# Gains applied at the split, weight splits ordered behind the norm chain, and fp32 GLU units in a hybrid S5 / latent-attention trunk

## The chip, the cores and the metric

The kernel runs on one core of one Trainium2 chip, as one launch. The metric is the device time of that launch in microseconds. The core has five engines with their own instruction queues: TensorE (PE in the profile, with its weight loads listed as PEld), VectorE (DVE), ScalarE (ACT), GpSimd (POOL) and SyncE (SP), which issues the DMA transfers. Each engine works through its queue in order.

## The reference

A residual stream x of 256 tokens by 2048 channels, fp32, goes through four sub-layers, each between two RMS norms with their own gains ("sandwich" norms):

```
x = x + norm(s5(norm(x, g00)), g01)      # state space, then a GLU: val * sigmoid(gate)
x = x + norm(ffn0(norm(x, g02)), g03)    # 2048 -> 5632 -> 2048, gated, causal conv of width 3
x = x + norm(attention(norm(x, g10), K/V from norm(x, kv_norm_g)), g11)
x = x + norm(ffn1(norm(x, g12)), g13)
```

with `norm(x, g) = x * rsqrt(mean(x*x) + 1e-6) * g`. The state-space mixer is a complex diagonal recurrence (128 groups of 16 channels, 64 states each) over the 256 tokens, a gelu, and `y @ w_glu + b_glu`, of which one half gates the other. The attention is a latent attention with 16 heads, rank 512 for queries and keys/values and a rotary part, masked by chunks of 64 tokens. All weights come as fp32 and are read once.

## The kernel before

The 256 tokens are two blocks of 128 (tb = 0 and 1). **Weight units.** Weights stream from HBM in units of 1 MB (`wunit`, L76): a transfer into `raw` (two buffers), then two halves of 128 x 1024, each split into a high and a low fp32r part: ACT copies the high part (L73, `whi`), DVE subtracts it from the fp32 value (L74, `wlo`). For a weight with a gain, L101 does the same per row. The units that span a change of stage go to named slots (`HOLD`, tiles `x...`) instead of the rotating `whi`/`wlo`. A product is three fp32r matmuls (`mm3`, L107 to L110: high x high, high x low, low x high) or two (`mm2`, L114, L115). Activations are split in the same way (`act` tiles, the transposed layout with channels on partitions, tokens in the free dimension).

**Stages.** The state-space stage (`s5`, until about 262 us) is a software pipeline over 16 state blocks: per block PE makes small products (L399, L467, L481, L497), DVE multiplies and runs the scan (L508), ACT copies out of PSUM. After every fourth block `part_d` (L545) turns four channel tiles of the result y and splits them; they are one quarter (`qt`) of the GLU's contraction. Each finished quarter puts four GLU weight units (`glu_early`, L243: two column blocks x two halves) into the list `todo`, and each later step of the pipeline takes one of them. What is left of the list, and the column blocks 2 and 3, run in `glu_rest` (L624). Then come `ffn(0)` (L684), `attention` (L818), `ffn(1)`.

**The change of stage.** When a stage ends, each token block goes through a chain. `finish_chunk` (L163) takes the sum of squares on ACT (L139) and multiplies the result f by the post-norm's gain on DVE (L166), four times 512 columns. `post_norm` (L168) makes the reciprocal root (`rstd1`, L141: sum L145, power on POOL L147, and three small DVE rows L149, L151, L153), adds to the residual (L172, four times), squares it (L139), and, where the next stage is an FFN, multiplies x by the next norm's gain into f (L178, four times). `pre_scale` (L180) makes a second reciprocal root and scales the identity by it (L182, tile `xh`). `pre_turn` (L185) turns the block by 16 fp32 matmuls with `xh` as the moving operand (L191), so that the norm's scale is applied by the turn itself, and splits the result (L192). The turn of block 0 runs before the next stage's first products; the turn of block 1 (`tail()`) runs after block 0's products of the first four (or, for the attention, held) units. The gain is a broadcast load of 1 MB (`gb`, L160).

**What sets the order.** The program is written in one order; a scheduler puts each engine's instructions into a fixed queue by the order of the program and by when their inputs would be ready in its model. So splits of the next stage's weights stand between the small rows of the chain on DVE.

Of the kernel before, what the change touches and what calls it, by code (L numbers as in the profile page):

```python
# [15 lines left out]
P = 128  # L16
D = 2048
# [27 lines left out]
def tile_trunk(ctx: ExitStack, tc: tile.TileContext, a: dict):  # L45
# [117 lines left out]
    def finish_chunk(f, fst, tb, n, g):  # L163
        c = f[tb][:, n * 512 : (n + 1) * 512]
        sq_acc(c, fst[tb][:, n : n + 1])
        dve.tensor_tensor(c, c, g[0][:, n * 512 : (n + 1) * 512], op=ALU.mult)  # L166

    def post_norm(f, fst, tb, x, xst, g):  # L168
        r = rstd1(fst[tb], D)
        for n in range(NCH):  # L170
            c = slice(n * 512, (n + 1) * 512)
            dve.scalar_tensor_tensor(x[tb][:, c], f[tb][:, c], r, x[tb][:, c], op0=ALU.mult, op1=ALU.add)  # L172
            if xst is None:
                sync.dma_start(a["out"][tb * P : (tb + 1) * P, c], x[tb][:, c])
                continue
            sq_acc(x[tb][:, c], xst[:, n : n + 1])
            if g is not None:
                dve.tensor_tensor(f[tb][:, c], x[tb][:, c], g[0][:, c], op=ALU.mult)  # L178

    def pre_scale(xst):  # L180
        d = T(env["ap"], [P, 512], F32, "xh", 2)[:, :P]
        dve.tensor_scalar(d, ident, rstd1(xst, D), None, op0=ALU.mult)  # L182
        return d

    def pre_turn(h, d, tb):  # L185
        for n in range(NCH):
            pt = accb()
            ptv = pt.rearrange("p (k t) -> p k t", t=P)
            for k in range(4):
                o = (4 * n + k) * P  # L190
                pe.matmul(ptv[:, k, :], h[:, o : o + P], d, start=True, stop=True)  # L191
            split(*acts4(tb, n, slice(0, 4)), ptv)  # L192

# [42 lines left out]
    def glu_mm(bank, b, tb, halves):  # L236
        hk, u = halves
        for i, (wh, wl) in enumerate(u):
            for k in range(hk):
                j = i * hk + k  # L240
                mm3(bank, *acts(tb, 4 * b + j), wh[:, k, :], wl[:, k, :], b == 0 and j == 0, b == 3 and j == 3)

    def glu_early(f, n, b, half):  # L243
        hv = glu_load(n, b, half)
        banks = [accb(), accb()]
        for tb in range(NB):
            hk, u = hv
            for i, (wh, wl) in enumerate(u):
                for k in range(hk):
                    j = i * hk + k  # L250
                    mm3(banks[tb], *acts(tb, 4 * b + j), wh[:, k, :], wl[:, k, :], j == 0, j == 3)
        o = half * 1024 + n * 512
        for tb in range(NB):
            c = f[tb][:, o : o + 512]
            if b == 0:
                act.activation(c, banks[tb], AF.Copy)
            else:
                dve.tensor_tensor(c, banks[tb], c, op=ALU.add)


    def s5(f):
        with tc.tile_pool(name="s5", bufs=2) as q1:
# [276 lines left out]

            def glu_steps(b):  # L540
                for n in range(2):
                    for half in range(2):
                        yield glu_early(f, n, b, half)

            def part_d(qt, yg):  # L545
                act_tiles()
                for hh in range(2):
                    ptv = wk().rearrange("p (t m) -> p t m", t=4)
                    for t in range(4):
                        pe.transpose(ptv[:, t, :], yg[:, 7 - (4 * hh + t), :], ident)  # L550

                    def av(z):
                        return z.rearrange("p j (c t) -> p t j c", t=8)[:, 4 * hh : 4 * hh + 4]

                    for tb in range(NB):
                        hi, lo = acts4(tb, qt, slice(0, 4))
                        split(av(hi), av(lo), ptv.rearrange("p t (j c) -> p t j c", j=4)[:, :, :, 16 * tb : 16 * tb + 16])

# [18 lines left out]
            for n in range(nb + 2):  # L577
                if 0 <= n - 1 < nb:
                    vs = part_v(U[n - 1], ET.pop(n - 1))
                if n >= 2:  # L580
                    m = n - 2
                    if m % PB == 0:
                        yg = T(q1, [P, 8, P], F32, "yg", 1)
                    part_c(m, yg, ab.pop(m)[1], U.pop(m), TP.pop(m), H.pop(m))
                if 0 <= n - 1 < nb:
                    R = part_r(n - 1, vs, *fr[n - 1])
                if n < nb:
                    U[n], TP[n] = part_k(n, *ab[n])
                    ET[n] = part_e(ab[n][0])
                if 0 <= n - 1 < nb:  # L590
                    H[n - 1] = part_h(n - 1, R, *fr.pop(n - 1))
                if n >= 2 and m % PB == PB - 1:
                    part_d(m // PB, yg)
                    todo.append(glu_steps(m // PB))
# [9 lines left out]
    sync.dma_start(gkv, a["gkv"])  # L604
    sync.dma_start(gq, a["gq"])
# [17 lines left out]

    def glu_rest(q1, todo, f, fst, gains, done):  # L624
        def finish(n, tb, banks, bb):
# [6 lines left out]
            dve.tensor_tensor(c, c, sg, op=ALU.mult)  # L632
            finish_chunk(f, fst, tb, n, gains[0])

# [11 lines left out]
        for n in range(2, 4):  # L646
            banks = [(wk if n % 2 == 0 else accb)() for _ in range(4)]
            held = []
            for b in range(4):
# [9 lines left out]
                if n == 2 and b < 2:  # L659
                    if b == 0:  # L660
                        gain_load(gains[0])
                    bb = bias(b)
                    for tb in range(NB):
                        finish(b, tb, None, bb)
                if n == 2 and b == 2:
                    load_x(x)
                if n == 3 and b == 0:
                    bb = bias(2)
                    for tb in range(NB):
                        finish(2, tb, pb, bb)  # L670
                    gain_load(gains[1])
# [12 lines left out]
    def ffn(l, tail, gains, f, fst, done):  # L684
        with tc.tile_pool(name=f"ff{l}", bufs=2) as q1:
# [42 lines left out]
            for part, npair in enumerate(PARTS):  # L728
                hid = []
                for pr in range(p0, p0 + npair):  # L730
                    banks = [wk(), wk()] if pr == 0 else [[wk(), wk()] for _ in range(2)]
                    held = []
                    for which, w in enumerate((wg, wu)):
                        for kh in range(2):
                            v = w[:, 8 * kh : 8 * kh + 8, pr * S : (pr + 1) * S]
                            if pr == 0:
                                held.append((which, kh, wunit(v, 8, S, slots=HOLD[len(held)])))
                            else:
# [36 lines left out]
                if part == len(PARTS) - 2:  # L775
                    for g in gains:
                        if g is not None:
                            gain_load(g)

# [4 lines left out]
                def evac(n, tb, bank):  # L784
# [5 lines left out]
                    if last:  # L790
                        finish_chunk(f, fst, tb, n, gains[0])

# [24 lines left out]

    def attention(tail, gains, f, fst, done):  # L818
        with tc.tile_pool(name="at", bufs=2) as q1:
# [34 lines left out]
            for which, (w, gain) in enumerate(((wdkv, gkv), (wdq, gq))):  # L854
                banks = [accb(), accb()]
                held = []
                for un in range(4):
                    hv = wunit(
                        w[:, 4 * un : 4 * un + 4, 0:RANK], 4, RANK, gain[:, 4 * un : 4 * un + 4],
                        slots=(None, None) if which else HOLD[un],  # L860
                    )
                    down(banks[0], un, 0, hv)
# [156 lines left out]

            for g in gains:  # L1020
                gain_load(g)
            for n in range(NCH):
# [8 lines left out]
                for tb in range(NB):  # L1031
# [6 lines left out]
                    act.activation(c, banks[tb], AF.Copy)  # L1038
                    finish_chunk(f, fst, tb, n, gains[0])
                    if held:  # L1040
# [19 lines left out]
    def begin(gpost, gpre, last=False, f=None):  # L1060
        f, fst, xst = f or f_pair(), [stats() for _ in range(NB)], [None if last else stats() for _ in range(NB)]
        gp = gain_tile(gpost)
        gn = None if gpre is None else gain_tile(gpre)

        dg = {}

        def done(tb, stage):
            if stage == 0:
                post_norm(f, fst, tb, x, xst[tb], gn)
# [5 lines left out]
        return (gp, gn), f, fst, done  # L1075

    with tc.tile_pool(name="gl", bufs=2) as q1:
        gs, f, fst, done = begin(ng[0, 1], ng[0, 2], f=f)
        tail = glu_rest(q1, todo, f, fst, gs, done)
        rope_tables(q1)  # L1080
    tail = ffn(0, tail, *begin(ng[0, 3], None))
    tail = attention(tail, *begin(ng[1, 1], ng[1, 2]))
    ffn(1, tail, *begin(ng[1, 3], None, True))


# [28 lines left out]
def _arrays(i):  # L1114
# [8 lines left out]
    def blocks(re, im):  # L1123
# [21 lines left out]
        "w_glu": g("ssm_w_glu")[0],  # L1145
        "b_glu": g("ssm_b_glu"),
        "gkv": pn(g("kv_norm_g")),
        "gq": pn(g("norm_g")[1, 0]),
# [30 lines left out]
```

## Time and profile before

| | |
|---|---|
| median of three runs | 2193.63 us (2193.27 to 2194.26) |
| profiled execution | 2187.58 us |
| its span, first to last instruction | 2185.8 us |
| mean granted TensorE clock | 0.990 |
| busy: PE, DVE, ACT | 2079.0 us (95%), 1408.8 us (64%), 1122.4 us (51%) |
| DMA | 374.74 MB, mean 171 GB/s |

A row of the order of time gives start, duration, engine, line, operation, `out<-in`, shapes, a count, and in brackets the idle time before it and what released it. A group row gives busy time, mean ns and the idle time before. A released wait names the last semaphore that came. An fp32 matmul stands in the records as two (x2 per matmul), so 16 matmuls of the turn are x32.

### The profile page before, as it was taken

Reading aid. Unit: us, or ns where it says so; the run is one execution under the profiler, and the core shown is the slowest. Engines: PE = TensorE matmul, PEld = TensorE weight load, DVE = VectorE, ACT = ScalarE, POOL = GpSimd, SP = SyncE. Lnnn points to the kernel's source line nnn. Section 1 sums busy time; section 2 is a strip of 40 time slices with the busy share of each in tenths; the row PEclk is TensorE's granted clock in tenths of the full one; section 3 lists DMA queues with packets and bytes.
Section 4 is the critical chain, followed back from the end, with each engine's and each line's share of the span. In section 5 each row is a group of like instructions: output and inputs, shape, how many; then the busy total and the mean of one; then the engine's idle time right before and its main releaser. Section 6 shows DMA issues by size and latency. Waiting matters only on the chain.

```text
span 2185.8 us, 32404 instructions
## 1 busy us (share of the span) xinstructions
PE 2079.0 (95%) x13268; PEld 1764.2 (81%) x13268; DVE 1408.8 (64%) x1940; ACT 1122.4 (51%) x1695; POOL 19.8 (1%) x57
## 2 busy tenths in 40 slices
PE   3788999899999999999989999989999999999998
PEld 2566777888888888888878998788888888888886
DVE  7999666666466556655686665566646655665567
ACT  6677445455455445544464554545545544554444
POOL 0000000000000000000000000000000000000000
PEclk9999999999999999999999999999999999999999
DMA  4132476455565555555564434635555555555654
GB/s 131 50 98 75 154 233 206 145 188 179 193 197 187 193 193 191 178 190 193 192 200 129 136 118 155 212 123 189 189 193 193 180 187 193 193 183 184 194 191 154
DMA packets 280966, 374.74 MB, mean 171 GB/s; under 512 B 9200, under 2 KB 196208, under 8 KB 279792
## 3 DMA queue, kind: packets, MB, share of 16 engines
q1 hardware_dynamic: 280816, 372.66, 52.4%
q8 instruction: 104, 1.70, 0.3%
q14 instruction: 46, 0.38, 0.1%
HBM read 370.54 MB, written 2.10 MB: 170 GB/s over the span
## 4 chain that ended last, share of the span: by engine, by line
PE 82%; DVE 10%; DMA 4%; ACT 3%; issue 1%; POOL 0%; SPq 0%; DVEq 0%; POOLq 0%; ACTq 0%
PE wk L114 29%; PE wk L115 15%; PE acc L108 9%; PE acc L109 9%; PE acc L110 9%; DMA raw<-in_w_glu 3%; PE wk L108 2%; PE wk L109 2%; PE wk L110 2%; DVE wlo L74 2%; PE acc L191 1%; DVE x L74 1%; ACT whi L73 1%; DVE f L431 1%; DVE f L430 1%
## 5 line engine op out<-in xcount | busy, mean ns | idle before, releaser
L74 DVE TENSOR_TENSOR wlo<-raw,whi 128x1024 fp32r<-128x1024 f32 (+2 forms) x640 | 761.0, 1191 | 584.0 <-ACT whi L73 579.3
L73 ACT ACTIVATE whi<-raw 128x1024 fp32r<-128x1024 f32 (+2 forms) x640 | 658.3, 1031 | 635.3 <-PE wk L114 245.6
L114 PE MATMUL wk<-act,whi 128*128 128x512 f32 x2688 | 941.9, 395 | 0.0
L115 PE MATMUL wk<-act,wlo 128*128 128x256 f32 x2688 | 753.0, 280 | 0.0
L114 PEld LDWEIGHTS wk<-act,whi 128*128 128x128 f32 x2688 | 504.1, 188 | 119.3
L115 PEld LDWEIGHTS wk<-act,wlo 128*128 128x128 f32 x2688 | 507.4, 189 | 0.3
L108 PE MATMUL acc<-whi,hh 128*128 128x512 f32 x652 | 255.4, 392 | 0.0
L109 PE MATMUL acc<-wlo,hh 128*128 128x512 f32 x652 | 255.3, 392 | 0.0
L110 PE MATMUL acc<-whi,hl 128*128 128x512 f32 x652 | 254.3, 391 | 0.0
L108 PEld LDWEIGHTS acc<-whi,hh 128*128 128x128 f32 x652 | 122.4, 188 | 27.2 <-ACT hh L73 0.5
L109 PEld LDWEIGHTS acc<-wlo,hh 128*128 128x128 f32 x652 | 122.4, 188 | 27.0 <-DVE wlo L74 0.5
L110 PEld LDWEIGHTS acc<-whi,hl 128*128 128x128 f32 x652 | 122.4, 188 | 26.9
L108 PE MATMUL acc<-whi,act 128*128 128x512 f32 (+1 forms) x332 | 126.4, 381 | 2.7 <-ACT act L73 2.7
L109 PE MATMUL acc<-wlo,act 128*128 128x512 f32 (+1 forms) x332 | 124.9, 377 | 1.9 <-DVE wlo L74 1.9
L110 PE MATMUL acc<-whi,act 128*128 128x512 f32 (+1 forms) x332 | 124.3, 375 | 0.1
L765 DVE SCALAR_TENSOR_TENSOR cv<-gs,cw,cv 128x255 f32<-128x255 f32 (+1 forms) x168 | 77.2, 480 | 3.0
L109 PEld LDWEIGHTS acc<-wlo,act 128*128 128x128 f32 x332 | 62.5, 188 | 14.9 <-DVE wlo L74 4.0
L108 PEld LDWEIGHTS acc<-whi,act 128*128 128x128 f32 x332 | 62.5, 188 | 14.5 <-ACT act L73 3.0
L110 PEld LDWEIGHTS acc<-whi,act 128*128 128x128 f32 x332 | 62.5, 188 | 11.5 <-DVE act L74 0.5
L763 ACT ACTIVATE cv<-gs,cb,cw 128x256 f32<-128x256 f32 x84 | 50.5, 601 | 36.5 <-DVE gs L715 36.5
L714 ACT ACTIVATE us<-wk 128x256 f32<-128x256 f32 x84 | 31.7, 380 | 60.3 <-PE wk L115 60.3
L714 ACT ACTIVATE gs<-wk 128x256 f32<-128x256 f32 x84 | 32.0, 381 | 59.8 <-PE wk L115 59.8
(282 smaller groups left out, 2342.5 us busy)
## 6 DMA issues: line engine op xcount, KB each, us to landing
raw<-in_w_gate SPq DMA_DIRECT2D x88, 1024.0 KB, 5.0
raw<-in_w_up SPq DMA_DIRECT2D x88, 1024.0 KB, 4.9
raw<-in_w_down SPq DMA_DIRECT2D x88, 1024.0 KB, 4.9
raw<-in_w_glu SPq DMA_DIRECT2D x32, 1024.0 KB, 6.2
raw<-in_w_o SPq DMA_DIRECT2D x16, 1024.0 KB, 4.9
raw<-in_w_ukv SPq DMA_DIRECT2D x8, 1024.0 KB, 5.3
gb<-in_norm_g SPq DMA_DIRECT2D x6, 1024.0 KB, 6.7
raw<-in_w_uq SPq DMA_DIRECT2D x8, 768.0 KB, 4.4
```

The costliest lines, as they stand in the source:

```text
L73: act.activation(hi, src, AF.Copy)
L74: (eng or dve).tensor_tensor(lo, src, hi.bitcast(F32), op=ALU.subtract)
L108: pe.matmul(o, lh, rh, start=first, stop=False)
L109: pe.matmul(o, lh, rl, start=False, stop=False)
L110: pe.matmul(o, ll, rh, start=False, stop=last)
L114: pe.matmul(ov, lh, r, start=first, stop=False)
L115: pe.matmul(ov[:, 0, :], ll, r[:, 0, :], start=False, stop=last)
L191: pe.matmul(ptv[:, k, :], h[:, o : o + P], d, start=True, stop=True)
L430: dve.tensor_tensor(f1, zt(0, 0, 9, 1), bc(2, 9), op=ALU.mult)
L714: act.activation(z[:, ft, :], two[ft][:, S:], AF.Copy)
L763: act.activation(cv[:, ft, :], gv[:, ft, :], AF.Identity, scale=cw[:, 2, n : n + 1], bias=cb[:, n : n + 1])
L765: dve.scalar_tensor_tensor(cv[:, ft, sh:], gv[:, ft, : S - sh], cw[:, 2 - sh, n : n + 1], cv[:, ft, sh:], op0=ALU.mult, op1=ALU.add,)
```

## The change

Three things change.

1. The next norm's gain is no longer multiplied into f ahead of the turn. x itself is turned in every case, and for the two FFNs the gain, now a per-partition scalar (`gf`, 128 x 16, loaded at the start of the program), is applied when the turned block is split: 16 ACT copies with a scale and 16 DVE `scalar_tensor_tensor` of 128 x 128 for each token block, in place of four and four of 128 x 512. The broadcast gain loads of these two norms go.
2. `behind(ins)` orders what is issued in it behind the instruction that scales the identity for block 0 (on the same engine, DVE): the post-gain multiply of block 1, the end of the GLU of block 1, and the low splits of the next stage's first units (in the FFN all but the first of the held four, in the attention the third and fourth of the first weight).
3. The GLU units of the first three quarters (12 of the 16 in `todo`) are not split. `glu_full` multiplies the raw fp32 weights with an fp32 copy of the turned activations (`ax`, one more ACT copy in `part_d`): 8 fp32 matmuls of 512 columns in place of 24 fp32r. The fourth quarter's stay split.

```diff
@@ finish_chunk, post_norm, pre_scale, pre_turn
-        dve.tensor_tensor(c, c, g[0][:, n * 512 : (n + 1) * 512], op=ALU.mult)
+        with behind(env["turn"] if tb else None):
+            dve.tensor_tensor(c, c, g[0][:, n * 512 : (n + 1) * 512], op=ALU.mult)
...
-            if g is not None:
-                dve.tensor_tensor(f[tb][:, c], x[tb][:, c], g[0][:, c], op=ALU.mult)
...
+    def behind(ins):
+        return nullcontext() if ins is None else tc.issue_after(ins)
+
+    def pre_turn(h, d, tb, g):
...
-            split(*acts4(tb, n, slice(0, 4)), ptv)
+            hi, lo = acts4(tb, n, slice(0, 4))
+            if g is None:
+                split(hi, lo, ptv)
+                continue
+            for k in range(4):
+                gk = g[:, 4 * n + k : 4 * n + k + 1]
+                act.activation(hi[:, k, :], ptv[:, k, :], AF.Copy, scale=gk)
+                dve.scalar_tensor_tensor(
+                    lo[:, k, :], ptv[:, k, :], gk, hi[:, k, :].bitcast(F32), op0=ALU.mult, op1=ALU.subtract
+                )
@@ new
+    def glu_full(f, n, b, half, ax):
+        raw = T(env["wp"], [P, 4, 512], F32, "raw")
+        col = half * D + n * 512
+        sync.dma_start(raw, glu_w[b][:, :, col : col + 512])
+        banks = [accb(), accb()]
+        for tb in range(NB):
+            for j in range(4):
+                pe.matmul(banks[tb], ax[:, j, tb * P : (tb + 1) * P], raw[:, j, :], start=j == 0, stop=j == 3)
+        glu_keep(f, n, b, half, banks)
@@ part_d, glu_steps
+                        yield glu_early(f, n, b, half) if ax is None else glu_full(f, n, b, half, ax)
...
+                ax = None if qt == 3 else T(q1, [P, 4, S], F32, "ax", 1)
...
+                        if ax is not None:
+                            act.activation(av(ax[:, :, tb * P : (tb + 1) * P]), src, AF.Copy)
@@ program start
+    gf = [T(cp, [P, KT], F32, f"gf{l}") for l in range(2)]
+    for l in range(2):
+        sync.dma_start(gf[l], a["gf"][l])
@@ glu_rest, ffn, attention
-            finish(3, tb, banks, bb)
+            with behind(env["turn"] if tb else None):
+                finish(3, tb, banks, bb)
...
-                                held.append((which, kh, wunit(v, 8, S, slots=HOLD[len(held)])))
+                                with behind(before if held else None):
+                                    held.append((which, kh, wunit(v, 8, S, slots=HOLD[len(held)])))
...
+                    with behind(before if which == 0 and un > 1 else None):
@@ begin
+        env["turn"] = None
...
-                    dg[tb] = pre_scale(xst[tb])
+                    dg[tb], ins = pre_scale(xst[tb])
+                    if tb == 0:
+                        env["turn"] = ins
             elif not last:
-                pre_turn((x if gn is None else f)[tb], dg[tb], tb)
+                pre_turn(x[tb], dg[tb], tb, gpre)
```

The lines of the new kernel are shifted: L145 to L153 stay, L166 becomes L167, L172 becomes L173, L182 becomes L181, L629 and L631 become L660 and L662; L201 is the new low split with the gain, L261 the fp32 matmul.

DVE's queue at the change from the GLU to `ffn(0)`, from block 0's first reciprocal root to its `xh` (`x_...` and `wlo` are low splits of the FFN's first units, `tot` the sum of squares, `sg` the gate of block 1). Before:

```order
L145 TENSOR_REDUCE tot_4044<-st_597_3290 128x1
L74 TENSOR_TENSOR x_792_4262<-raw_4260,x_792_4262 128x1024
...
L74 TENSOR_TENSOR x_793_4265<-raw_4260,x_793_4265 128x1024
L153 SCALAR_TENSOR_TENSOR rs_r_741_4052<-rs_u_740_4050,rs_y_738_4046 128x1
L172 SCALAR_TENSOR_TENSOR x_3285<-f_84,rs_r_741_4052,x_3285 128x512 x2
L178 TENSOR_TENSOR f_84<-x_3285,gb_3295 128x512 x2
...
L74 TENSOR_TENSOR x_795_4270<-raw_4268,x_795_4270 128x1024
...
L74 TENSOR_TENSOR wlo_4274<-raw_4268,whi_4273 128x1024
L153 SCALAR_TENSOR_TENSOR rs_r_751_4080<-rs_u_750_4078,rs_y_748_4074 128x1
L166 TENSOR_TENSOR f_85<-f_85,gb_3294 128x512
L182 TENSOR_SCALAR xh_4070<-cst_73,rs_r_751_4080 128x128
```

And in the changed kernel:

```order
L145 TENSOR_REDUCE tot_3773<-st_558_3045 128x1
L149 TENSOR_SCALAR rs_m_695_3777<-tot_3773 128x1
L151 SCALAR_TENSOR_TENSOR rs_u_696_3779<-rs_m_695_3777,rs_y_694_3775 128x1
L153 SCALAR_TENSOR_TENSOR rs_r_697_3781<-rs_u_696_3779,rs_y_694_3775 128x1
L173 SCALAR_TENSOR_TENSOR x_3040<-f_88,rs_r_697_3781,x_3040 128x512 x4
L145 TENSOR_REDUCE tot_3797<-st_560_3047 128x1
...
L181 TENSOR_SCALAR xh_3795<-cst_73,rs_r_707_3805 128x128
L660 TENSOR_TENSOR sg_3920<-acc_3536,bias_3624 128x512
L74 TENSOR_TENSOR x_748_4007<-raw_4005,x_748_4007 128x1024
L662 TENSOR_TENSOR f_89<-acc_3534,bias_3624 128x512
L201 SCALAR_TENSOR_TENSOR act_220_1125<-acc_3868,gf_6_78,act_220_1125 128x128
```

The chain of block 0 now stands alone up to `xh`; the low splits, block 1's bias rows and the 16 new gain splits come behind it and ahead of block 1's own `xh`.

ACT's queue near the start of the state-space stage (`whi` are high splits of the first GLU units, `TP` and `vs` copies that the pipeline's next products read). Before:

```order
L73 ACTIVATE whi_1167<-raw_1165 128x1024
L419 ACTIVATE bc_469<-bc_469,cst_73 128x128
L73 ACTIVATE whi_1171<-raw_1165 128x1024
L73 ACTIVATE whi_1355<-raw_1353 128x1024
L473 ACTIVATE TP_288<-acc_289 128x512
```

And in the changed kernel:

```order
L506 ACTIVATE ET_329<-wk_336 128x512
L443 ACTIVATE bc_473<-bc_473,cst_73 128x128
L497 ACTIVATE TP_292<-acc_293 128x512
L497 ACTIVATE TP_292<-acc_294 128x512
L512 ACTIVATE vs_376<-wk_367 128x2x128
```

The three splits that stood ahead of the copies are gone with the units' split form.

More of the change, by code (lines that the diff above doesn't have):

```diff
@@ L1 @@
 import math
-from contextlib import ExitStack
+from contextlib import ExitStack, nullcontext
 import concourse.bass as bass
@@ L251, in glu_early, with glu_keep @@
                     mm3(banks[tb], *acts(tb, 4 * b + j), wh[:, k, :], wl[:, k, :], j == 0, j == 3)
+        glu_keep(f, n, b, half, banks)
+    def glu_keep(f, n, b, half, banks):
         o = half * 1024 + n * 512
@@ L622, in rope_tables, with glu_rest @@
         sincos(rsin, rcos, rr, rn, cst[:, C_RS : C_RS + 1])
-    def glu_rest(q1, todo, f, fst, gains, done):
+    def glu_rest(q1, todo, f, fst, gain, done):
         def finish(n, tb, banks, bb):
@@ L632, in finish @@
             dve.tensor_tensor(c, c, sg, op=ALU.mult)
-            finish_chunk(f, fst, tb, n, gains[0])
+            finish_chunk(f, fst, tb, n, gain)
         def bias(n):
@@ L660, in glu_rest @@
                     if b == 0:
-                        gain_load(gains[0])
+                        gain_load(gain)
                     bb = bias(b)
@@ L670, in glu_rest @@
                         finish(2, tb, pb, bb)
-                    gain_load(gains[1])
                     bb = bias(n)
@@ L678, in glu_rest, with ffn @@
                 done(0, 1)
-            finish(3, tb, banks, bb)
+            with behind(env["turn"] if tb else None):
+                finish(3, tb, banks, bb)
             done(tb, 0)
         return lambda: done(1, 1)
-    def ffn(l, tail, gains, f, fst, done):
+    def ffn(l, tail, before, gain, f, fst, done):
         with tc.tile_pool(name=f"ff{l}", bufs=2) as q1:
@@ L775, in ffn @@
                 if part == len(PARTS) - 2:
-                    for g in gains:
-                        if g is not None:
-                            gain_load(g)
+                    gain_load(gain)
                 def load(n, un, slots=(None, None)):
@@ L790, in evac @@
                     if last:
-                        finish_chunk(f, fst, tb, n, gains[0])
+                        finish_chunk(f, fst, tb, n, gain)
                 if last:
@@ L815, in ffn, with attention @@
         return lambda: done(1, 1)
-    def attention(tail, gains, f, fst, done):
+    def attention(tail, before, gpost, f, fst, done):
         with tc.tile_pool(name="at", bufs=2) as q1:
@@ L857, in attention @@
                 for un in range(4):
[L858 to L861, printed above, removed]
+                    with behind(before if which == 0 and un > 1 else None):
+                        hv = wunit(
+                            w[:, 4 * un : 4 * un + 4, 0:RANK], 4, RANK, gain[:, 4 * un : 4 * un + 4],
+                            slots=(None, None) if which else HOLD[un],
+                        )
                     down(banks[0], un, 0, hv)
@@ L1018, in attention @@
                     q = {"kv": kv, "qn": qn, "qr": rope(q1, qs_, br[:, S:])}
-            for g in gains:
-                gain_load(g)
+            gain_load(gpost)
             for n in range(NCH):
@@ L1038, in attention @@
                     act.activation(c, banks[tb], AF.Copy)
-                    finish_chunk(f, fst, tb, n, gains[0])
+                    finish_chunk(f, fst, tb, n, gpost)
                     if held:
@@ L1146, in _arrays @@
         "b_glu": g("ssm_b_glu"),
+        "gf": np.stack([pn(g("norm_g")[l, 2]) for l in range(2)]),
         "gkv": pn(g("kv_norm_g")),
```

30 lines of the change are left out of this document (14 added, 16 removed).

## The prediction

> **What bounds the kernel now.** I first read the page's chain of waits, then the busy time by stretches, then each engine's order of time where a stretch has gaps. All times are of the profiled execution (2187.58 us); the median of the runs is 2193.63 us, so the sum below is a difference that I add to the median.
>
> The chain that ended last, shares of the span:
>
> ```profile
> PE 82%; DVE 10%; DMA 4%; ACT 3%; issue 1%; POOL 0%; SPq 0%; DVEq 0%; POOLq 0%; ACTq 0%
> ```
>
> TensorE (PE) carries the span; the other 18% lie in few places. Stretches from 93 us on (columns: from:to, length, then busy us and count of PE, PE weight load, DVE, ACT, POOL, then granted clock, DMA share, GB/s):
>
> ```profile
> 93.00:235.00 142.00, 122.89 (x1993) 93.14 (x1999) 132.21 (x211) 105.64 (x197) 0.25 (x4) 1.00 0.28 79
> 235.00:262.00 27.00, 26.81 (x277) 21.36 (x262) 16.57 (x26) 11.67 (x18) 0.00 (x0) 1.00 0.43 132
> 262.00:300.00 38.00, 34.78 (x146) 26.67 (x145) 29.69 (x38) 18.31 (x25) 0.00 (x0) 0.99 0.87 289
> 300.00:386.00 86.00, 83.51 (x351) 65.78 (x349) 52.38 (x64) 41.63 (x51) 0.59 (x2) 0.98 0.68 204
> 386.00:432.00 46.00, 38.74 (x294) 37.82 (x295) 26.99 (x49) 19.04 (x35) 3.54 (x5) 0.89 0.38 131
> ...
> 40.00:50.00 10.00, 5.55 (x60) 4.12 (x68) 6.55 (x11) 5.18 (x14) 0.00 (x0) 0.67 0.25 72
> 390.00:400.00 10.00, 6.76 (x38) 6.76 (x39) 9.78 (x20) 4.64 (x11) 2.28 (x3) 0.58 0.70 243
> 1140.00:1150.00 10.00, 4.66 (x24) 4.66 (x25) 9.89 (x23) 8.53 (x22) 1.98 (x4) 0.66 0.77 217
> 1420.00:1430.00 10.00, 2.60 (x12) 2.02 (x11) 9.86 (x20) 5.29 (x12) 2.83 (x3) 0.79 0.40 138
> ```
>
> In the state-space stage (93 to 235) DVE is busy 132.2 of 142 us and PE idles 19.1: both engines are near the bound, DVE nearer. From 235 to 386 PE idles 0.2 + 3.2 + 2.5 us. Each of the three changes of stage holds a hole: around 395, 1145 and 1425 DVE is full (9.8 to 9.9 of 10) while PE waits, and the granted clock drops to 0.58, 0.66 and 0.79. The rows of PE that end these holes, and the turn of the second token block:
>
> ```profile
> 393.24 6.28 PE L191 MATMUL acc<-xh,f 128*128 128x128 f32 x32 [7.29 <-DVE xh L182]
> 410.76 3.73 PE L191 MATMUL acc<-xh,f 128*128 128x128 f32 x32
> ...
> 1145.34 4.82 PE L191 MATMUL acc<-xh,x 128*128 128x128 f32 x24 [5.92 <-DVE xh L182]
> ...
> 1428.87 5.61 PE L191 MATMUL acc<-xh,f 128*128 128x128 f32 x32 [7.41 <-DVE xh L182]
> ```
>
> 7.29, 5.92 and 7.41 us of waiting for the scaled identity xh. The turn behind the first takes 6.28 us for 32 records, the second turn 3.73: the half clock costs another 2.5.
>
> **Part 1: the fp32 units.** Twelve GLU units drop two ACT and two DVE splits each and issue 8 fp32 matmuls in place of 24. What they issue now in 93 to 235 (groups by line: busy, mean ns, idle before), and how closely matmuls follow each other, split form at 265 us and fp32 form in the scores at 1227 us:
>
> ```profile
> L108 PE MATMUL acc<-whi,act 128*128 128x512 f32 x64 | 26.4, 412 | 2.7 <-ACT act L73 2.7
> ...
> L74 DVE TENSOR_TENSOR wlo<-raw,whi 128x1024 fp32r<-128x1024 f32 x16 | 19.4, 1220 | 4.3 <-ACT whi L73 4.3
> L73 ACT ACTIVATE whi<-raw 128x1024 fp32r<-128x1024 f32 x16 | 16.8, 1053 | 5.6 <-PE acc L110 5.6
> ```
>
> ```profile
> 265.10 0.39 PE L108 MATMUL acc<-whi,act 128*128 128x512 f32 x1
> ...
> 265.78 0.39 PE L108 MATMUL acc<-whi,act 128*128 128x512 f32 x1
> ...
> 1226.68 0.60 PE L951 MATMUL acc<-knT,qnT 128*128 128x256 f32 x2
> 1227.11 0.59 PE L952 MATMUL acc<-krE,rpo 128*128 128x256 f32 x2
> ```
>
> Three split matmuls take 265.78 - 265.10 = 0.68 us, so a unit 8 x 0.68 = 5.45. One fp32 matmul of 256 columns takes 1227.11 - 1226.68 = 0.43 us, of 512 then 0.86, a unit 6.9. That is +1.45 per unit. No row has an fp32 matmul of 512 columns; the nearest by form, the turn's 3.73 us for 16 matmuls of 128 columns, gives 0.93 per 512, so +1.45 to +2.0; I take the wider rows, 1.45. [...]
>
> 64 L108 in 93 to 235 are 8 units: PE rises there by 8 x 1.45 = 11.6 to 134.5; DVE falls by 19.4 to 112.8; ACT loses 16.8 and gains some 3 for the copy ax. The bound goes from DVE's 132 to PE's 134.5, and what decides is how much of PE's 19.1 us of idle is left. Those waits hang on DVE and ACT results that now come sooner. If 10 us stay, the stretch is 144.5, **+2.5**. Ends: 5 left, -2.5; all 19.1 left, +11.6.
>
> At the start of the stage ACT stands in its fixed order before work that PE wants:
>
> ```profile
> 42.09 1.06 ACT L73 ACTIVATE whi<-raw 128x1024 fp32r<-128x1024 f32 x1 [1.90 <-DMA raw<-in_w_glu]
> 43.05 1.07 ACT L473 ACTIVATE TP<-acc 128x512 f32<-128x512 f32 x2
> ...
> 44.45 0.48 PE L497 MATMUL wk<-cst,vs 128*128 128x128 f32 x1 [5.46 <-ACT vs L488]
> ```
>
> The weight split of 42.09, waiting for its transfer, stands ahead of the copy TP, and PE waits 5.46 us for what follows. The split is gone; DVE, busy 6.55 of 10 us there, can win back up to 3.45. I take -3.0, +0.9 for the two gain loads put at the head of SP's queue (issues there are 0.44 apart), and -0.6 for ACT's four splits in all that leave this place: **-2.7** (ends -4 and +0.9).
>
> ```profile
> 0.74 0.38 SPq L604 DMA_DIRECT2D gkv<-in_gkv  x1
> 1.18 0.41 SPq L605 DMA_DIRECT2D gq<-in_gq  x1
> ```
>
> From 235 on PE is full, so the other four fp32 units cost 4 x 1.45 = 5.8. One more thing comes: an fp32 unit reads raw until its last matmul, and there are two raw buffers, so the next transfer starts up to 6.9 us later, and the quarter behind it must again fill the split path. ACT already waits there for transfers:
>
> ```profile
> L73 ACT ACTIVATE whi<-raw 128x1024 fp32r<-128x1024 f32 x38 | 40.1, 1058 | 55.4 <-DMA raw<-in_w_glu 30.8 <-PE acc L110 15.2 <-PE wk L110 9.4
> ```
>
> One split pair, 1.05 + 1.22, is the refill: +2.3, and up to 5 with the transfer. Against it, 20 units between 265 and 386 take 121 us where 20 x 5.45 = 109 would do; an earlier start of transfers can give back some of these 12. I take 5.8 + 2.3 - 5.7 = **+2.4** (ends -4 and +11).
>
> **Part 2: gains at the split and the order behind xh.** At the first change of stage, DVE and GpSimd (POOL) stand so:
>
> ```profile
> 381.99 0.21 DVE L151 SCALAR_TENSOR_TENSOR rs_u<-rs_m,rs_y 128x1 f32<-128x1 f32 x1
> ...
> 383.44 1.41 DVE L172 SCALAR_TENSOR_TENSOR x<-f,rs_r,x 128x512 f32<-128x512 f32 x2
> 384.77 1.29 DVE L178 TENSOR_TENSOR f<-x,gb 128x512 f32<-128x512 f32 x2
> ...
> 391.09 1.22 DVE L74 TENSOR_TENSOR wlo<-raw,whi 128x1024 fp32r<-128x1024 f32 x1
> 392.30 0.69 DVE L166 TENSOR_TENSOR f<-f,gb 128x512 f32<-128x512 f32 x1
> 392.90 0.28 DVE L182 TENSOR_SCALAR xh<-cst,rs_r 128x128 f32<-128x128 f32 x1
> ...
> 405.39 0.29 DVE L182 TENSOR_SCALAR xh<-cst,rs_r 128x128 f32<-128x128 f32 x1
> ...
> 380.04 0.55 POOL L147 TENSOR_TENSOR rs_y<-tot,cst 128x1 f32<-128x1 f32 x1 [273.01 <-DVE tot L145]
> 389.33 1.45 POOL L147 TENSOR_TENSOR rs_y<-tot,cst 128x1 f32<-128x1 f32 x1 [8.70 <-DVE tot L145]
> ```
>
> Between pow (ends 380.6) and xh the new order has only the chain itself: three small rows (0.6), four L172 (2.75), the last square (0.8), sum, pow (0.55 with DVE free, 1.45 if not) and three small rows (0.8): 386.1 to 387. PE's wait of 7.29 us shrinks to about 1, and the turn runs at 3.7 instead of 6.28. But the work is only moved. Behind xh now queue six splits (6 x 1.22), three bias rows (2.0), L166 (0.7), and 16 gain splits of 128x128 (about 0.28 as L182 has it, 4.5), then the chain of the second block (some 6): 386.2 + 20.4 is 406. The second turn's xh, which came at 405.39 and was not waited for (the turn began at 410.76), thus stays where it is and becomes what PE waits for: turn at 406 to 407 instead of 410.76. I take **-3.5** (ends -5 and 0; the lower end would need the third weight unit's transfer on time). Two of the gain loads of 1 MB go; they lie off the path.
>
> At the second change only two rows leave the chain, 1143.54 and 1144.40:
>
> ```profile
> 1143.54 0.68 DVE L166 TENSOR_TENSOR f<-f,gb 128x512 f32<-128x512 f32 x1
> 1144.40 0.69 DVE L166 TENSOR_TENSOR f<-f,gb 128x512 f32<-128x512 f32 x1
> ```
>
> **-1.0** (0.6 to 2.5, with some of the half clock gone). At the third, ACT's order still pins the last square of the block:
>
> ```profile
> 1423.14 0.62 ACT L139 ACTIVATE junk<-x 128x512 bf16<-128x512 f32 x1
> ...
> 1425.15 0.15 DVE L145 TENSOR_REDUCE tot<-st 128x1 f32<-128x5 f32 x1
> ```
>
> The sum may follow at 1423.9, xh then at 1425.2 where it was 1428.53; the turn begins 3.4 us earlier and gains up to 1.9 in clock, of which a second wait as above takes some: **-2.7** (ends -4.5 and -0.5).
>
> [...]
>
> **Sum:** -2.7 + 2.5 + 2.4 - 3.5 - 1.0 - 2.7 = -5.0, so 2193.63 - 5.0 = **2188.6 us** (the profiled execution near 2182.6).
>
> **Rivals.** (B) The state-space stage is a DVE stage, and its relief is worth more. For it: 132 of 142 busy. Then PE's idle there falls to 2 (134.5 + 2 - 142 = -5.5) and the late transfers absorb the rest of the units' price (0): -2.7 - 5.5 + 0 - 7.2 = -15.4, 2178 us. Against it: PE's 134.5 leaves little room, and the scan's chain runs over PE, ACT and DVE in turn. (C, the other side) PE is the bound in this stage: its idle is latency of that chain and stays, so 12 x 1.45 = 17.4 lands on the path, and the refill with it. With 17 of the possible 19.7 for 93 to 386: -2.7 + 17 - 7.2 = +7.1, 2201 us. It decides slower from 14.3 on (14.3 - 9.9 = 4.4). For it: PE runs at 99% from 235 to 262. Against it: rows of PE's idle end in DVE and ACT results. (D) The second block's wait takes the whole place of the first at all three changes, halved clock included, since the same DVE rows must run before the second xh; the transitions then give 0 to -2 and the sum is about -0.5 + 2.2 - 2.7 = -1, 2192.6 us. For it: DVE is full in these 10 us stretches and keeps nearly all of its work. Against it: 5.1 us of slack ahead of 410.76.
>
> **How the numbers follow.** Forecast 0.50, B 0.17, C 0.17, D 0.16. A measurement of this kernel tells about 0.2% (4.4 us) from no change. The forecast's -5.0 lies just beyond, and its terms have ends of several us: 0.33 of its 0.50 count as faster, 0.17 as same. B is faster (0.17); D counts 0.14 same and 0.02 faster; C 0.13 slower and 0.04 same. Faster 0.52, same 0.35, slower 0.13. The range goes from B's 2178 to 2199, between D and C.
>
> **What would show it.** Right: PE's idle in 93 to 235 near 10 us and the stretch near 144; no wait of PE around 42 us; first turns waited for 1 to 3 us at full clock, second turns waited for at the first change. Wrong: the stage's end moving by more than 10 us either way; the second turn at 410 or later; xh still behind splits; an fp32 unit that takes other than 6.9 us.

## The result and the profile after

The changed kernel takes 2205.7 us (median of four runs, 2204.65 to 2206.95) where the kernel before took 2193.95 beside it: ratio 1.0045, 95% interval 1.0029 to 1.0062, so 6 to 14 us slower. The forecast was 2188.6 us, range 2178 to 2199: the wrong side, and outside the range. What came is rival C: PE pays for the fp32 units and nothing gives it back.

The profiled executions are 2187.58 us before and 2204.65 after, 17 us apart. The profile before lies 6 us under the median of its kernel, the one after on it, so the two profiles show some 5 us more than the runs do; where a stage of the two differs by 2 us or less I don't read anything from it.

The page of the changed kernel:

```profile
PE 2101.8 (95%) x13172; PEld 1750.8 (79%) x13172; DVE 1382.8 (63%) x1948; ACT 1106.4 (50%) x1723; POOL 17.7 (1%) x57
...
PE 82%; DVE 9%; DMA 4%; ACT 3%; issue 1%; POOL 0%; SPq 0%; DVEq 0%; POOLq 0%; ACTq 0%
...
L261 PE MATMUL acc<-raw,ax 128*128 128x512 f32 x192 | 86.1, 601 | 1.4 <-ACT ax L584 1.4
```

DVE and ACT lost 26 and 16 us of work, PE gained 23, and the shares of the chain hardly moved. Equal stretches of the clock hold different work in the two kernels, so I cut by work: from the fifth of the sixteen scans to the last, and from the last scan to the last GLU product ahead of the norm. Before (columns: from:to, length, then busy us and count of PE, PE weight load, DVE, ACT, POOL, then granted clock, DMA share, GB/s):

```profile
93.20:246.80 153.60, 134.49 (x2142) 102.44 (x2142) 137.60 (x220) 110.06 (x205) 0.25 (x4) 1.00 0.26 76
246.80:385.30 138.50, 132.65 (x603) 104.26 (x602) 92.34 (x115) 66.28 (x82) 0.59 (x2) 0.99 0.73 227
```

After:

```profile
92.30:257.60 165.30, 149.06 (x2066) 90.48 (x2067) 116.49 (x200) 87.92 (x188) 0.25 (x4) 0.98 0.25 71
257.60:404.40 146.80, 136.71 (x581) 98.99 (x581) 87.26 (x111) 64.14 (x84) 0.70 (x3) 1.00 0.70 219
```

Between the scans PE's busy time rises by 14.6 us, DVE's falls by 21, ACT's by 22, and the time rises by 11.7. PE's time that is not busy goes from 19.1 to 16.2: it did not shrink with DVE's load. The granted clock of the stretch is 1.00 before and 0.98 after. (1 - clock) x length is an estimate of the clock time that was not granted: about 3 us after and none before, so up to 3 of the 11.7 can be the clock. Behind the last scan PE is busy 4.1 us longer and not busy 10.1 instead of 5.9 us. One step of the state-space pipeline after shows why; PE first, then DVE (start, duration, in brackets the idle time before and its releaser):

```profile
131.72 7.03 PE L261 MATMUL acc<-raw,ax 128*128 128x512 f32 x16
138.68 0.64 PE L423 MATMUL wk<-ET,U 128*32 128x128 f32 x16
...
144.26 1.96 PE L491 MATMUL acc<-K,cst 64*32 64x256 f32 x64 [0.79 <-DVE K L476]
```

```profile
134.84 0.42 DVE L546 TENSOR_TENSOR H<-w,w 128x248 f32<-128x248 f32 x1
140.48 1.36 DVE L454 TENSOR_TENSOR f<-z,bc 128x1152 f32<-128x1152 f32 x1 [5.22 <-PE wk L423]
```

The unit takes 138.68 - 131.72 = 6.96 us, as the forecast had it. DVE is done at 135.3, halfway through the unit, and then waits 5.22 us, because the small products that it needs (L423, from 138.68 on) stand behind the unit in PE's queue. Once they have run, DVE takes from 140.48 to the end of L476 at 144.20, 3.7 us, for the next step's inputs, and PE waits for that (L491 for L476, 0.79 us). The splits taken from DVE left a hole under the unit, not a shorter step. Grouped over the stage (waited for: us in total, times, longest; L282 adds a unit's result to f):

```profile
DVE f L454 <- PE wk L423: 16.3, 7, 5.2
DVE f L282 <- PE acc L261: 16.0, 7, 3.0
...
PE acc L491 <- DVE K L476: 6.4, 9, 1.2
PE wk L521 <- DVE act L74: 3.5, 2, 2.1
```

At the changes of stage, the rows that answer to those of the prediction (first turn, then PE's next wait, for each change that has one):

```profile
405.65 3.84 PE L193 MATMUL acc<-xh,x 128*128 128x128 f32 x32 [0.60 <-DVE xh L181]
411.80 0.39 PE L108 MATMUL acc<-x,act 128*128 128x256 f32 x1 [2.31 <-DVE act L201]
...
1158.83 3.57 PE L193 MATMUL acc<-xh,x 128*128 128x128 f32 x15 [4.79 <-DVE xh L181]
...
1442.58 6.15 PE L193 MATMUL acc<-xh,x 128*128 128x128 f32 x32 [4.26 <-DVE xh L181]
1450.36 0.39 PE L108 MATMUL acc<-x,act 128*128 128x256 f32 x1 [1.62 <-DVE act L201]
...
400.00:410.00 10.00, 8.89 (x55) 7.47 (x53) 8.26 (x19) 8.07 (x20) 0.54 (x1) 1.00 0.30 103
411.00:415.00 4.00, 3.20 (x20) 3.20 (x21) 4.00 (x13) 2.49 (x8) 0.69 (x1) 0.78 0.76 253
1438.00:1448.00 10.00, 5.74 (x29) 5.42 (x28) 4.87 (x12) 5.43 (x13) 1.97 (x3) 0.66 0.02 3
```

At the first change the wait of 7.29 us is 0.60, and the turn runs at full clock (1.00 from 400 to 410) in 3.84 us instead of 6.28. At the third the wait falls from 7.41 to 4.26 and the turn still takes 6.15 us at a clock of 0.66. At both a new wait stands behind the turn, 2.31 and 1.62 us, for the narrow gain splits L201. Behind the one of 2.31 us the clock drops as well (0.78 from 411 to 415), and with one of 2.42 us in e3 below (0.66 from 395 to 400); the wait of 4.79 us at the second change comes with a clock of 0.50 from 1157.33 to 1164.16. The drop doesn't always come: in the kernel before, PE waits 2.71 and 2.84 us between the scans (at 102.24 and 153.72), and the clock of that stretch is 1.00.

To compare the three changes over all kernels I took the time from the start of PE's idle ahead of the first turn to the 200th matmul record behind the second turn, where the same work has been done:

| kernel | first | second | third |
|---|---|---|---|
| before | 57.4 | 66.0 | 56.9 |
| three more kernels with this code unchanged (e1, e5, e6) | 56.6 to 56.8 | 66.3 to 66.8 | 56.8 to 57.7 |
| order only (e3) | 57.7 | 64.7 | 54.9 |
| gain only (e4) | 58.9 | 66.5 | 56.3 |
| both, split units (e2) | 53.4 | 64.5 | 57.2 |
| both, later first splits (e8) | 52.8 | 65.6 | 55.3 |
| the changed kernel | 52.7 | 65.6 | 56.8 |
| both, gain left out (e9) | 51.3 | 65.7 | 54.6 |

### The profile page after: what moved, and what is told of

The parts are those of the page before. It is cut to its first block, busy times and chain, and to the rows that moved or that the text cites. A ratio compares the mean times of both kernels' runs of the same rounds, so it can differ in the third digit from the quotient of the medians.

```text
span 2202.9 us, 32219 instructions
## 1 busy us (share of the span) xinstructions
PE 2101.8 (95%) x13172; PEld 1750.8 (79%) x13172; DVE 1382.8 (63%) x1948; ACT 1106.4 (50%) x1723; POOL 17.7 (1%) x57
## 4 chain that ended last, share of the span: by engine, by line
PE 82%; DVE 9%; DMA 4%; ACT 3%; issue 1%; POOL 0%; SPq 0%; DVEq 0%; POOLq 0%; ACTq 0%
PE wk L114 28%; PE wk L115 14%; PE acc L109 9%; PE acc L108 9%; PE acc L110 9%; PE acc L261 3%; DMA raw<-in_w_glu 2%; PE wk L108 2%; PE wk L109 2%; PE wk L110 2%; DVE wlo L74 1%; PE wk L423 1%; DVE f L455 1%; PE acc L193 1%; DVE f L454 1%
## 5 line engine op out<-in xcount | busy, mean ns | idle before, releaser
L74 DVE TENSOR_TENSOR wlo<-raw,whi 128x1024 fp32r<-128x1024 f32 (+1 forms) x616 | 731.6, 1190 | 577.0 <-ACT whi L73 574.2
L73 ACT ACTIVATE whi<-raw 128x1024 fp32r<-128x1024 f32 (+1 forms) x616 | 632.6, 1030 | 624.2 <-PE wk L114 244.4
L109 PE MATMUL acc<-wlo,act 128*128 128x512 f32 (+1 forms) x236 | 87.4, 371 | 3.0 <-DVE wlo L74 3.0
L108 PE MATMUL acc<-whi,act 128*128 128x512 f32 (+1 forms) x236 | 87.0, 371 | 1.0 <-ACT whi L73 0.8
L261 PE MATMUL acc<-raw,ax 128*128 128x512 f32 x192 | 86.1, 601 | 1.4 <-ACT ax L584 1.4
L110 PE MATMUL acc<-whi,act 128*128 128x512 f32 (+1 forms) x236 | 86.7, 368 | 0.0
L261 PEld LDWEIGHTS acc<-raw,ax 128*128 128x128 f32 x192 | 36.7, 193 | 42.8 <-issue 40.7
L108 PE MATMUL acc<-x,act 128*128 128x256 f32 (+1 forms) x148 | 50.7, 345 | 4.3 <-DVE act L201 3.9
```

Source lines behind the costliest of these rows:

```text
L73: act.activation(hi, src, AF.Copy)
L74: (eng or dve).tensor_tensor(lo, src, hi.bitcast(F32), op=ALU.subtract)
L108: pe.matmul(o, lh, rh, start=first, stop=False)
L109: pe.matmul(o, lh, rl, start=False, stop=False)
L110: pe.matmul(o, ll, rh, start=False, stop=last)
L261: pe.matmul(banks[tb], ax[:, j, tb * P : (tb + 1) * P], raw[:, j, :], start=j == 0, stop=j == 3)
```

## The experiments

All ratios are to the kernel before, run beside them on the same chip, with 95% intervals. Theory 1: the state-space stage is carried by PE and by its chain of small steps; the fp32 units' price lands on the path. Theory 2: part 3 is free and the order behind the norm chain costs.

**e1: part 3 alone.** The kernel before with `glu_full`, the copy `ax` and `glu_keep` of the diff, nothing else.

> Part 3 alone (12 GLU units as fp32 matmuls), gains and order as before. Theory 1 (the state-space stage is bound by PE and by the latency of its chain, so the dearer matmuls land on the path and the splits taken from DVE and ACT bring nothing): +13 to +18 us, all of it between 93 and 400 us; 253 us in the kernel before (last product of the state blocks) comes near 265. Theory 2 (part 3 is about free, and the loss comes from the order behind the norm chain): within 4 us of before.

Measured: 1.0067 (1.0055 to 1.008), 14.7 us slower. The last product of the state blocks comes at 263.8 us. Theory 2 falls.

**e2: parts 1 and 2 alone.**

```diff
-                ax = None if qt == 3 else T(q1, [P, 4, S], F32, "ax", 1)
+                ax = None
```

> Parts 1 and 2 alone (gains at the split, order behind xh), all 16 GLU units of the list split as before. Theory 1: faster than before by 2 to 6 us (first change of stage -5, second -0.3, third +2, as the trace of the changed kernel reads). Theory 2: slower than before by 5 us or more, like the changed kernel.

Measured: 0.9971 (0.9958 to 0.9984), 6.4 us faster. With e1 this adds up to 1.0038, and the whole change measured 1.0045: the parts are about additive. The forecast for the three changes of stage (-7.2) is near this in sum; by the table they give -4.0, -1.5 and +0.3.

**e3 and e4: order alone, gain alone.** e3 is the kernel before with the `behind` lines of the diff; e4 is e2 with

```diff
-        return nullcontext() if ins is None else tc.issue_after(ins)
+        return nullcontext()
```

> Part 2 alone: the order behind xh, the next norm's gain still multiplied into f ahead of the turn. If the order is what empties the first wait: the 7.29 us at the first change falls to about 3 (the four gain multiplies of 0.6 us stay in the chain) and the time to -1 to -4 us. If the order costs at the third change (the second block's turn 2.4 us later against the first): the same +2 there.

> Part 1 alone: gains at the split, no order behind xh. The splits stay between the rows of the chain, so the first wait falls only by the four gain multiplies, 7.3 to about 4.5 us, and the second turn is not delayed: 0 to -3 us. If the 2.4 us lost at the third change come from the 16 small gain splits rather than from the order, they show here too.

Measured: 0.9996 (0.9987 to 1.0005) and 1.0006 (0.9997 to 1.0015): neither is told from no change, though together they give 0.3%. For e3 I had expected 1 to 4 us less. The first change, PE in e3 and then in e4:

```profile
394.46 5.47 PE L195 MATMUL acc<-xh,f 128*128 128x128 f32 x32 [2.42 <-DVE xh L183]
...
395.00:400.00 5.00, 5.00 (x32) 5.00 (x31) 3.33 (x5) 2.46 (x5) 0.00 (x0) 0.66 0.00 0
...
412.71 0.58 PE L109 MATMUL acc<-wlo,act 128*128 128x256 f32 x1 [2.63 <-DVE wlo L74]
```

```profile
396.32 6.72 PE L193 MATMUL acc<-xh,x 128*128 128x128 f32 x32 [7.52 <-DVE xh L181]
414.43 3.73 PE L193 MATMUL acc<-xh,x 128*128 128x128 f32 x32
```

Order alone takes the first wait to 2.42 us, but the turn still runs at 0.66 of the clock (5.47 us), and then PE waits for the weight splits that were pushed back, 2.63 us in this row: the table's 57.7 is no gain. With the gain taken out of the chain but the splits left in it the wait is 7.52, not the 4.5 expected: the scheduler filled the freed places with splits (four L74 of 1.22 us stand between the end of L173 at 388.96 and xh at 395.98; before, two stand between the last L178 and xh). My expectation for e4 was wrong there.

**e5: DVE relieved, PE unchanged.**

```diff
-                split(hi, lo, raw[:, h : h + hk, :], pool if slots[i] in onpool else None)
+                if env.get("nolo"):
+                    act.activation(hi, raw[:, h : h + hk, :], AF.Copy)
+                    lo = hi
+                else:
...
+        env["nolo"] = b < 3
```

> The kernel before with the DVE half of the weight split taken away alone: in the 12 units of the first three quarters the low part is not computed and the high part stands in its place in the same 24 matmuls (the low part of these weights is left out of the result). DVE loses 24 x 1.22 = 29 us before 262 us, ACT and PE keep everything. If DVE bounds the state-space stage (rival B of the prediction): -10 us or more. If PE and the latency of its chain bound it: 0 to -4 us, and PE's busy time over the block products from the fifth scan to the last stays 134 us with 15 to 19 us not busy.

Measured: 0.999 (0.998 to 1.0), 2 us faster and 4 at most. The stretch from the fifth to the last scan, and that of e2, which has the same clock and all its splits:

```profile
94.30:253.50 159.20, 139.23 (x2147) 106.20 (x2145) 115.90 (x194) 102.73 (x198) 0.25 (x4) 0.97 0.26 75
...
95.40:251.50 156.10, 138.97 (x2146) 105.83 (x2145) 137.69 (x220) 110.17 (x205) 0.25 (x4) 0.97 0.26 75
```

DVE falls from 137.6 to 115.9 us, and the stretch takes 159.2, against 153.6 to 156.2 in the six kernels with whole split units and unchanged matmuls (before, e2, e3, e4, e8, e9); the expected 134 us of PE were 139, as in e2, at a clock of 0.97. At this clock 22 us less of DVE did not shorten the stretch. DVE's 90% was not the bound. Rival B falls.

**e10: PE relieved, DVE unchanged.**

```diff
-                    mm3(banks[tb], *acts(tb, 4 * b + j), wh[:, k, :], wl[:, k, :], j == 0, j == 3)
+                    lh, ll = acts(tb, 4 * b + j)
+                    if b == 3:
+                        mm3(banks[tb], lh, ll, wh[:, k, :], wl[:, k, :], j == 0, j == 3)
+                    else:
+                        pe.matmul(banks[tb], lh, wh[:, k, :], start=j == 0, stop=False)
+                        pe.matmul(banks[tb], lh, wl[:, k, :], start=False, stop=j == 3)
```

> The kernel before, with PE relieved instead of DVE: in the 12 units of the first three quarters the third matmul (high weight by low activation) is left out of the result, 16 matmuls instead of 24, 1.8 us less PE per unit, 22 us in all; DVE and ACT keep all. If PE carries these stages: 10 us or more off, and the time from the fifth to the last scan (154 to 156 us with split units) falls to about 145. If DVE carries the state-space stage: there 0 to -3 us, and only the units behind the last scan (about 3 x 1.8 us) come off.

Measured: 0.9945 (0.9931 to 0.9959), 12 us faster for 22 us less of PE.

```profile
94.10:243.90 149.80, 126.33 (x2071) 92.91 (x2071) 137.04 (x221) 102.97 (x199) 0.25 (x4) 0.94 0.27 78
243.90:378.90 135.00, 127.71 (x578) 97.83 (x577) 91.69 (x115) 65.81 (x82) 0.58 (x2) 1.00 0.76 233
```

The whole fits theory 1. The stretch between the scans, 149.8, lies between the two expectations (145, and 151 or more): 4 to 6 us of the 16 taken from PE there come off, and behind it 3.5 (138.5 to 135.0) of the 4.9 that PE's busy time lost. So PE carries it, but not alone: taken from PE, a microsecond of this stretch gives back a third here (and half from e6 to e11, below), taken from DVE nothing. Two things take the rest. PE waits for DVE's K 10.0 us in all (L472 for L457), where the kernel before has 1.1. And the clock is 0.94: by the same estimate, (1 - clock) x length, about 9 us of clock time are not granted, against none before. How much of the 16 a full clock would have given back, no run shows.

**e6: the refill.** Part 3 alone, with the raw weights in the slots of the split parts:

```diff
-        raw = T(env["wp"], [P, 4, 512], F32, "raw")
+        raw = [T(env["wp"], [P, 2, 512], F32, "w" + v, env["wb"]) for v in ("hi", "lo")]
...
+        for i in range(2):
+            sync.dma_start(raw[i], glu_w[b][:, 2 * i : 2 * i + 2, col : col + 512])
```

> Part 3 alone, but the raw fp32 weights go to the slots that the split parts had, so that the two raw buffers are free for the fourth quarter's transfers. If the refill of the split path (4.2 us of PE not busy behind the last fp32 unit) and the buffers held to the last matmul cost what the trace reads: 4 us less than part 3 alone (+0.67%), about +0.45 to +0.5%. If only the dearer matmuls cost: no change against part 3 alone.

Measured: 1.0032 (1.0022 to 1.0043), against e1's 1.0067: 0.35%, 7.7 us. From the last scan to the last GLU product it takes 142.0 us where e1 takes 147.7 (e6, then e1):

```profile
256.50:398.50 142.00, 136.40 (x583) 100.65 (x582) 88.94 (x113) 63.49 (x79) 1.61 (x2) 0.99 0.64 204
...
256.60:404.30 147.70, 138.29 (x583) 100.20 (x582) 89.17 (x113) 62.75 (x79) 1.62 (x2) 0.99 0.71 219
```

The changed kernel takes 146.8. So about half of part 3's price is that an fp32 unit holds a raw buffer to its last matmul, and the split units behind it start late: the first two of their transfers are issued at 273.0 and 279.9 us in the changed kernel, at 31.9 and 33.8 in e6. PE's time that is not busy here is 5.9 us before, 9.4 in e1 and 5.6 in e6. PE of the changed kernel at that place:

```profile
280.32 0.73 PE L108 MATMUL acc<-whi,act 128*128 128x512 f32 x2 [0.49 <-ACT whi L73]
...
288.82 0.50 PE L109 MATMUL acc<-wlo,act 128*128 128x512 f32 x1 [1.05 <-DVE wlo L74]
...
PE wk L108 <- ACT whi L73: 2.4, 2, 2.2
```

**e11: fp32 units with PE's work of before.** e6, and

```diff
-            for j in range(4):
+            for j in (0, 2, 3):
```

> The fp32 units with own buffers, with 6 of their 8 matmuls (a quarter of the contraction of these units is left out of the result): 6 x 0.86 = 5.2 us of PE per unit against 5.45 of the split form, so about PE's work of before, with DVE's and ACT's splits gone. If the dearer matmuls are the price: fifth to last scan falls from 165 to 151 to 155 us, the whole to -0.1 to -0.4% against before, what is left of a gain being the start of the stage (4 us). If something else of the fp32 form costs (loads of fp32 weights, the copy ax): it stays above before.

Measured: 0.9978 (0.9968 to 0.9989). From e6 to e11 PE loses 12 x 2 x 0.86 = 20.6 us and the kernel 0.54%, 11.9 us. The stretch between the scans falls from 165.5 to 157.3, which misses the expected 151 to 155:

```profile
91.30:248.60 157.30, 138.22 (x2031) 87.04 (x2031) 116.50 (x199) 88.80 (x190) 0.25 (x4) 0.95 0.26 77
```

It is no shorter than with split units: 21 us less on each of DVE and ACT show no gain there at about equal PE. The clock is 0.95, about 8 us not granted by the estimate, so at a full clock the stretch could be some us under the split kernels; no run shows that. What is left of a gain is the start: the first scan at 44.7 us instead of 49.9.

**e8: the start without the fp32 price.** e2, and

```diff
-        hv = glu_load(n, b, half)
+        with behind(env["tp"] if b == 0 else None):
+            hv = glu_load(n, b, half)
```

> Parts 1 and 2 without part 3, and the first quarter's split units put behind the copy TP of the first block on ACT, which is what part 3 did at the start of the stage (first scan 45.6 us where it was 49.9). Theory: the start's 4 us come without the fp32 price, so 3 to 5 us less than parts 1 and 2 alone (-0.29%), about -0.45%. Rival: the splits only move into the next blocks, where DVE is full, and nothing is left: -0.29%.

Measured: 0.9955 (0.9943 to 0.9967), median 2186.16 us: 3.5 us below e2, the expected size, though the two intervals overlap, and the fastest kernel here that computes the whole. First scan 45.8 us, fifth 92.8 (e2: 50.7 and 95.4).

**e9: the narrow gain splits.** e2, and `if g is None` in `pre_turn` always taken.

> Parts 1 and 2 without part 3, with the FFN norms' gain left out: the turned block is split by 4 wide instructions per engine as before instead of 16 narrow ones. If the 2.3 us and 1.6 us that PE waits behind the first turn for L201 are the price of the 16 narrow splits, both fall below 0.5 and the time is 2 to 5 us below parts 1 and 2 alone. If it is DVE's place in the queue (bias rows and weight splits ahead of them): they stay.

Measured: 0.9969 (0.9956 to 0.9981), against e2's 0.9971: by time not told apart, below the 2 to 5 us expected. In the trace the waits for the splits behind the first turns are gone, but at the first change PE waits 2.79 us at the second turn instead. The table has 51.3 and 54.6 where e2 has 53.4 and 57.2. I leave open whether the narrow splits cost the kernel anything.

**e12: units in two halves.** e8, with each unit's 24 matmuls issued as 12 and 12 at two places of a step:

```diff
+            if tb == 0:
+                yield
...
                     ET[n] = part_e(ab[n][0])
+                if todo and next(todo[0], True) is True:
+                    todo.pop(0)
```

> Parts 1 and 2 with the later first splits, and every split unit of the list issued in two halves (12 matmuls for block 0, 12 for block 1) at two places of a step of the pipeline instead of one run of 24. If PE's 15 to 19 us of not busy time between the fifth and the last scan are waits for the chain's latency that a unit at the right place covers: 3 to 8 us less than the same kernel with whole units (-0.45%). If the step is full (PE 13.5, DVE 13 of 14 us): no change.

Measured: 0.9998 (0.9989 to 1.0007), 9.4 us slower than e8. My expectation was wrong in sign.

```profile
91.90:257.10 165.20, 143.35 (x2153) 105.60 (x2154) 138.12 (x220) 107.73 (x202) 0.25 (x4) 0.96 0.26 75
...
DVE f L286 <- PE acc L110: 9.2, 3, 4.9
DVE wlo L74 <- ACT whi L73: 7.8, 5, 4.5
```

165.2 us between the scans instead of e8's 154.8. DVE waits 9.2 us for the units' own products (L286 adds a unit's result to f; 1.9 us in e8) and 7.8 us for ACT's high splits (6.1 in e8). The clock is 0.96 where e8 has 0.99, an estimate of 5 us more not granted. The stage is sensitive to where a unit stands in PE's queue; how the 9.4 us divide between the order and the clock was not shown.

## Why the prediction was wrong

| step | predicted | measured (profiles) |
|---|---|---|
| start, to the fifth scan | -2.7 | -0.9 |
| state-space stage | +2.5 | +11.7 (fifth to last scan) |
| from there to the norm | +2.4 | +8.3 |
| first change of stage | -3.5 | -4.7 |
| second | -1.0 | -0.4 |
| third | -2.7 | -0.1 |

Together +13.9; the other 3 us of the 17 between the spans lie between these places, where nothing is changed. The stretches of the table are cut by work, the prediction's by time, so its second and third rows are best read as one: +4.9 predicted, +20.0 measured.

**The step that failed is "If 10 us stay".** The price of a unit was right (6.9 predicted, 6.96 measured), and so was PE's rise (11.6 predicted for eight units, 14.6 measured with 148 fp32 records, 9.25 units, in the stretch). Wrong was what I let the idle time do. I wrote that PE's waits "hang on DVE and ACT results that now come sooner" and that half of them would go; the case "all 19.1 left, +11.6" stood as an end of the term. The waits did move to other places, but in sum stayed (19.1 to 16.2), because, as in the step above, the results come sooner only while PE is in the unit. e5 shows that DVE's relief shortens nothing between the scans, e11 that both reliefs show no gain there, and e10 that PE's work counts. Reading the stage from the busy shares (DVE 132 of 142, so DVE is the bound) was the mistake: the step is a loop through both engines, and a unit in PE's queue is a fixed piece of it. A count of one step's rows could have warned me: in the kernel before, the step from 129.63 to 143.16 us leaves PE 0.5 us free, so a dearer unit had no room in it. It could not have named the bound, since DVE is as full there (13.49 of 13.53 us). That took runs that relieve one engine at a time.

The sum also had no term for the granted clock between the scans. The stretch stood at 1.00 in the profile before and at 0.94 to 0.99 in most others, so a stage's time in one profile carries some us of clock, and the +11.7 of the table up to 3.

**The refill was sized too small.** I took +2.3 and set -5.7 against it for transfers that would start earlier. e6 puts the whole effect of the held buffers at 7.7 us, by intervals that allow about 4 to 11. The transfers don't start earlier, they start later (the first two at 273.0 and 279.9 us, in e6 at 31.9 and 33.8), since the buffer is freed by the last matmul and no longer by a split; I had said this, and still credited the opposite.

**The start** was the right mechanism: ACT's split ahead of TP cost 4.3 us at the first scan (49.9 to 45.6, e8 45.8), a little more than the 3.45 that I capped it at, but 3.4 of them are gone again at the fifth scan.

**The changes of stage** were right in sum by time (-7.2 predicted; e2 measured -6.4, and the table gives -5.2 for e2 and for the changed kernel) and wrong in their parts. The first came as worked out, and a little better: the turn at full clock, and the second turn not waited for (it begins at 424.83, its xh is ready at 424.69), so rival D falls. The third gave nothing in the profile of the changed kernel: its first wait fell by 3.15 us as predicted, but the clock was 0.50 again, from 1440.64 to 1447.47, and L201 took 1.6 us behind the turn, a wait that my sum had only for the second turn. I had costed the 16 narrow splits as queue time in front of block 1, never as what the first product waits for. That a shorter wait gives the clock back was my estimate, from the 6.28 and 3.73 us of the two turns; it held at a wait of 0.60 us and not at 4.26.

**The rivals.** C is the case that came: its 2201 us were short of 2205.7 since it had the refill inside 17 us, and the start and the third change at full value. I gave it 0.17. The sum of D counts the start twice: -0.5 + 4.9 - 2.7 is +1.7, or 2195.3 us, not -1.

## What to carry to other kernels

Where two engines are both near 90% busy in a stage, relieve one at a time before calling either the bound, and compare stretches at the same granted clock: in this loop over in-order queues, work taken from the engine that was not in the way only made a hole (5.22 us of DVE in the step above). An operation that drops a preparation step may hold its input buffer longer than the step did (7.7 us here, e1 against e6); price the transfers behind it, not just the arithmetic. Parts that each show nothing alone (order, gain) can be worth 0.3% together: here the order alone left a first wait of 2.42 us with a lower clock, the gain alone one of 7.52, and only both brought it to 0.60.

## What the runs showed of the hardware that I had not expected

Waits of 2.42 us (e3) and 4.26 us (third change) ahead of the turn's 32 short fp32 records both came with a lower clock (0.66 from 395 to 400 and from 1438 to 1448) and cost 1.6 and 2.3 us in the turn (5.47 and 6.15 against 3.84); at 0.60 us the clock stayed at 1.00 (400 to 410). In the profiles of the kernel before and of the changed kernel the lower clock is 0.50 each time, for 3.41 us (299.39 to 302.81 before, 413.23 to 416.64 after), 6.83 (1440.64 to 1447.47 after) or more (10.24, from 388.14 to 398.38 before). From 40 us on, these two profiles have eight waits of PE of 3.38 to 7.4 us, and in each of them such a drop begins. Of their nine waits between 2.0 and 2.9 us, three have a drop that begins 0.3 to 1.7 us behind them (2.90 us before; 2.12 and 2.31 after), and six have none there, among them the 2.71 and 2.84 us above. So a wait of this length came with 1.6 us more in one place (e3) and with a full clock in another, and shortening a long wait to 2 to 3 us does not make sure of the clock. The other surprise is that leaving out a third of these units' matmuls (e10) returned just over half of PE's time.
